# A two-layer trunk on one core: the u projection moved last, compression weights six ahead, phasor sums on VectorE, five projection banks

## The chip, the core and the metric

The kernel runs on one core of a Trainium2 chip. The metric is the device time of one execution in microseconds (us); the kernel before takes 1839.51 us in the median of 3 runs (1838.10 to 1841.22). Each core has a matrix engine (TensorE, PE in the rows), a vector engine (VectorE, DVE), a scalar engine (ScalarE, ACT), GpSimd (POOL) and a sync engine (SP) that issues most loads. Every engine works through its own instructions in order and waits for others at semaphores.

## What is computed

A decoder trunk of two layers on 512 positions of width 1024, in float32. One combined projection feeds three token mixers; their outputs are gated and merged, and an MLP follows:

```python
for l in range(DEPTH):
    h = rmsnorm(x, norm_mix[l])
    proj = h @ w_in[l]
    q_a, kv_a, g_a, q_b, kv_b, u_c, g_m = jnp.split(proj, splits, axis=-1)
    ...
    y_a = nsa_attention(q_a, k_a, v_a, gates_a, nsa_cmp_pos[l], nsa_cmp_w1[l], nsa_cmp_w2[l])
    ...
    y_b = banded_attention(q_b, k_b, kv_b[:, :, 1], B_WINDOW, swa_sinks[l]).reshape(bsz, seq, B_WIDTH)
    y_c = s5_layer(u_c, s5_a_re[l], ...)
    g_m = jax.nn.sigmoid(g_m.reshape(bsz, seq, N_BRANCH, D_MODEL))
    merged = (g_m[:, :, 0] * (y_a @ w_branch_a[l])
              + g_m[:, :, 1] * (y_b @ w_branch_b[l])
              + g_m[:, :, 2] * (y_c @ w_branch_c[l]))
    x = x + merged @ w_out[l]
    h = rmsnorm(x, norm_mlp[l])
    x = x + jnp.square(jax.nn.relu(h @ w_mlp_up[l])) @ w_mlp_down[l]
return rmsnorm(x, norm_final)
```

`nsa_attention` compresses keys and values of overlapping blocks with a small two-layer network (`nsa_cmp_w1`, `nsa_cmp_w2`); `s5_layer` is a diagonal state-space recurrence, whose tables depend on parameters alone.

## The kernel before, in words

Every float32 product is made of three products: both factors are split into a high and a low half (`hh`, `hl` for the activations; `wh`, `wl` for a weight tile). The high half of a weight is a copy by ScalarE (L138, L146). The low half is either a subtraction on VectorE (`split`, L147) or, with `"add"`, the negated weight written by ScalarE (L137) to which an accumulating DMA, issued by GpSimd, adds the weight again (`split_add`, L139). Raw tiles `wr` have 2 buffers, `wh` and `wl` 3 each.

**The front of a layer** is five projections of 512 positions, one after another through `proj_tok` (L584 to L610): wkv01 (keys and values of two branches), wu (input of the recurrence), wkv2 (third branch, gates and the banded keys; 408 columns), wqb and wqa (queries). Each has four weight pieces `kp`; under each piece four tiles of 128 positions `t`; under each of these six matmuls into the tile's PSUM bank (tag `mm`, 4 banks), so one piece is 24 matmuls. After each group of six, `tick()` advances the background generators. At the end the four banks are evacuated: keys and queries by `rope` on VectorE (three operations), values by `v_split`, gates by a tanh on ScalarE, u by a ScalarE copy (L724). The next projection takes the same banks.

**In the background** run three generators. `turn()` transposes the keys and ends in `compress` (L1073 to L1118): 16 small weights `cw`, each for two matmuls of 65 columns into a bank `y`, eight for the keys and eight for the values; after each eight come a gelu and a small second matmul into another bank `y`, copied and split into `kst` or `vcst`. The weights are loaded three ahead into four buffers on SP's queue (`load_cw1`, L1068). In layer 0 `s5_prep` (L434 to L581) builds the tables of the recurrence in four quarters. A quarter has two steps. The first makes `wpn` and `wpnt` (products of powers, 128x1024), joined by an accumulating DMA (L520), and the phasors `E` and `Et` (L533 to L537), joined by another (L538) and stored as `cs`. The second multiplies `wpn` on TensorE (L563), copies it to `wi` and stores it as `win`, and makes `mo` and `mot` (L517, L518), joined and stored. The tiles wpn, wpnt, wi, mo and mot share four buffers (tag `pw`). `PD` gives the ticks: 9 to the start, 16 to the first quarter, 10 between the steps of a quarter; 1 tick lies between two quarters.

Attention follows at once: `q_stack` (L923) copies a query tile to `qd` on ScalarE, transposes it on TensorE, and splits it into `qh` (ScalarE, L933) and `ql` (VectorE, L934); scores and the filling gate matmuls (L153 to L155) come next.

The order on each engine is set by a scheduler when the program is built: it may move an instruction ahead of one that it takes to be late. On the chip each engine keeps that order.

Of the kernel before, what the change touches and what calls it, by code (L numbers as in the profile page):

```python
# [9 lines left out]
F32 = mybir.dt.float32  # L10
# [9 lines left out]
TT = S // 128  # L20
NEG = -1e38
STB = 0
PD = 9, 16, 10
NP = 8
EPS = 1e-6

# [37 lines left out]
class Trunk:  # L64
# [223 lines left out]
        self.yp = self.yp_cm.__enter__()  # L288

    def last_turn(self, tag):  # L290
        self.pins = [self.norm_turn(TT - 1, c, self.xlast[c], tag) for c in range(2)][1]

    def norm_turn(self, t, c, xg, tag):
        nc = self.nc
# [7 lines left out]
    def first_norm(self, pa):  # L302


        nc, I, tc = self.nc, self.I, self.tc
        ctx = ExitStack()
        xp, p = (ctx.enter_context(tc.tile_pool(name=n, bufs=1, reuse_waits="tile")) for n in ("xp", "nrm"))
        self.x = [xp.tile([128, D], F32, name=f"x{t}") for t in range(TT)]
        raw = []
        for t in range(TT):  # L310
            nc.sync.dma_start(self.x[t], I["x"][t * 128:(t + 1) * 128])
            if t == 0:
                self.norm_begin(p, I["norm_mix"][0])
                self.setup()
            elif t < 3:
                raw.append(self.raw(I["wkv01"][0, t - 1], 2, 512))
        nc.sync.dma_start(self.c, I["consts"])

        w = p.tile([128, 512], F32R, name="warm")
        nc.vector.memset(w.bitcast(F32), 0.0)  # L320
        b = self.bank("mm")
        for i in range(12):
            nc.tensor.matmul(b, w[:, 0:128], w, start=i == 0, stop=i == 11)
        xg, pre = [], []

        def gained(t):
            with self.after(self.pins):
                self.norm_sum(t, 0)
                self.norm_sum(t, 1)
                r = self.norm_rstd(t)  # L330
                xg.append([self.norm_half(t, c, r) for c in range(2)])

        def lead(t):
            if t < 2:
                with self.after([self.pow_done]):
                    pre.append(self.split(raw[t], nc.gpsimd))
            self.pins = [i for c in range(2) for i in self.norm_turn(t, c, xg[t][c], "y")] + [self.pow_done]
            if t + 2 < TT:
                gained(t + 2)
            if t == STB:  # L340
                with self.after(self.pins):
                    init.append(next(steps))
            if t == TT - 1:
                ctx.close()
                with self.after(self.pins):
                    self.rope_tables()

        self.pins = []
        gained(0)
        self.pins = [self.xg_done]  # L350
        gained(1)
        init, steps = [], self.s5_init(0, pa)
        with self.after([self.xg_done, self.sq_done]):
            next(steps)
        return lead, pre, init


# [76 lines left out]
    def s5_prep(self, l, init=None):  # L434
# [8 lines left out]
        with tc.tile_pool(name="prep", bufs=1, side="right", reuse_waits="tile") as p:  # L443
# [15 lines left out]

            V.tensor_scalar(PH[:, 1], PH[:, 1], self.sg, None, op0=OP.mult)  # L460
            if acc:
                PN = p.tile([128, 32, 8], F32, name="PN")
                V.tensor_scalar(PN, PH[:, 1, 1], -1.0, None, op0=OP.mult)
                NI = p.tile([128, 9, 32], F32, name="NI")
                V.tensor_scalar(NI, PI, -1.0, None, op0=OP.mult)
            loaded, nl = [], 2
# [15 lines left out]
            for q in range(4):  # L482
# [42 lines left out]
                wp_ = powers((X[:, 0], X[:, 1]), 1, "wpn")  # L525

                E = p.tile([128, 2, 8, 8, 8], F32, name="E", tag="E", bufs=nb)
                Et = p.tile([128, 2, 8, 8, 8] if acc else [128, 8, 8, 8], F32, name="Et", bufs=nb)
                eng = V
                se = [128, 8, 8, 8]  # L530
                hr, hi = (PH[:, x, 1, gs][:, :, :, None].to_broadcast(se) for x in range(2))
                lr, li = (PH[:, x, 0, gs][:, :, None, :].to_broadcast(se) for x in range(2))
                eng.tensor_tensor(E[:, 0], hr, lr, op=OP.mult)  # L533
                eng.tensor_tensor(E[:, 1], hr, li, op=OP.mult)
                if acc:
                    eng.tensor_tensor(Et[:, 0], PN[:, gs][:, :, :, None].to_broadcast(se), li, op=OP.mult)
                    eng.tensor_tensor(Et[:, 1], hi, lr, op=OP.mult)  # L537
                    nc.gpsimd.dma_start(E, Et, accum_op=OP.add)  # L538
                else:
                    eng.tensor_tensor(Et, hi, li, op=OP.mult)  # L540
                    eng.tensor_tensor(E[:, 0], E[:, 0], Et, op=OP.subtract)
                    eng.tensor_tensor(Et, hi, lr, op=OP.mult)
                    eng.tensor_tensor(E[:, 1], E[:, 1], Et, op=OP.add)

                def put(cs_d=cs_d, E=E):
                    nc.gpsimd.dma_start(cs_d, E.rearrange("p two g a b -> p two g (a b)"))

                if not acc:
                    put()
                V.tensor_tensor(ed, ed, self.c[:, None, C_E:C_E + 16].to_broadcast(sh), op=OP.mult)  # L550
                pins.close()
                if q < 3:
                    load(q + 1)
                yield PD[2]
                if acc:
                    put()

                wi = p.tile([128, 8, 128], F32, name="wi", tag="pw" if acc else "wi", bufs=4 if acc else 1)
                for g0 in (0, 3, 6):
# [15 lines left out]
                if not acc:  # L575
                    put()
                    put = lambda: None
                yield 1
            if acc:
                yield PD[2]  # L580
                put()  # L581


# [65 lines left out]
    def mixing(self, l, h):  # L649
        tc = self.tc  # L650
        with ExitStack() as right:
            def pool(name, side="right"):
                return tc.tile_pool(name=name, bufs=1, side=side, reuse_waits="tile")

            if l:
                right.push(self.yp_cm)
            with pool("qkv", "left") as self.qkv:
                with pool("pj", "left") as pj, self.banks(mm=4, s=1, t=1, y=2):
                    merged = self.q_pools(right, pool)
                    if l == 0:  # L660
                        pa = pool("pa")
                        *start, init = self.first_norm(pa.__enter__())
                    else:
                        start = [lambda t: t == TT - 1 and self.last_turn("y")]
                    self.project_init(l, pj)
                    if l == 0:
                        self.spawn(self.s5_prep(0, init), PD[0])
                    self.project_kv01(l, h, pj, *start)
                    self.project_u(l, h, pj)
                    self.project_kv2(l, h, pj)  # L670
                    self.project_qb(l, h, pj)
                    self.project_qa(l, h, pj)
                    self.drain()
                    if l == 0:
                        pa.__exit__(None, None, None)
                        self.y_pool()
                        right.push(self.yp_cm)
                self.ybp = right.enter_context(pool("ybp"))
                yb = [self.ybp.tile([128, 4, S], F32R, name=n, tag=n) for n in ("ybh", "ybl")]
                with pool("att", "left") as p, self.banks(mm=2, s=2, t=2, q=1, y=1):  # L680
                    ga = []
                    fill = self.fill(l, h, yb, merged, ga)
                    ya = self.attention(l, p, yb, self.yp, fill)
                    self.dump(f"yb{l}", yb[0].bitcast(F32))
                    self.dump(f"ya{l}", ya[0].bitcast(F32))
            with pool("post", "left") as p, self.banks(mm=4, s=1, t=1, y=2):
                self.scan_branch(l, h, p, fill, ya, ga, merged)
            with self.banks(mm=8):
                return self.w_out(l)
# [335 lines left out]
    def project_kv01(self, l, h, p, lead=None, pre=()):  # L1025
# [19 lines left out]

        def turn():
            self.cw1 = []
            for w in range(3):
                self.load_cw1(l, p, w)
            for t in range(TT):  # L1050
                kd, v0 = kds[t]
# [14 lines left out]
        self.proj_tok(h, self.I["wqa"][l], 512, self.evac_q(p, "qa"))  # L1066

    def load_cw1(self, l, p, w):  # L1068
        w1 = p.tile([128, 2, 128], F32, name="cw1", tag="cw1", bufs=4)
        self.nc.sync.dma_start(w1, self.I["cw1"][l, w // 8, w // 2 % 4][:, 2 * (w % 2):2 * (w % 2) + 2])  # L1070
        self.cw1.append(w1)

    def compress(self, l, p):  # L1073
# [7 lines left out]
        for j in range(2):  # L1081
            bh = self.bank("y")
            for w in range(8):
                if 8 * j + w < 13:
                    self.load_cw1(l, p, 8 * j + w + 3)
                if w % 2 == 0:
                    yield 2
                w1 = w1s[8 * j + w]
                for i in range(2):
                    ii = 2 * w + i  # L1090
                    nc.tensor.matmul(bh[:, 0:65], w1[:, i], ck[j][:, 2 * ii:2 * ii + 1025:16], start=ii == 0, stop=ii == 15)
# [303 lines left out]
    def mlp(self, l, h):  # L1395
# [3 lines left out]
        with tc.tile_pool(name="mlp", bufs=1, reuse_waits="tile") as p, self.banks(mm=7, t=1):  # L1399
# [3 lines left out]
            for fc in range(4):  # L1403
                act = []
                for f in range(8):
                    if (fc, f) in steps:
                        next(prep, None)
                    if not later:
# [3 lines left out]
                        for a, z in ((0, S - 128), (S - 128, S)) if len(two) > 1 else ((0, S),):  # L1412
                            for w, b in parts:
                                for kt in range(KT):
                                    if z < S and b is parts[1][1] and kt == 3:
                                        self.last_turn("t")
                                    self.mm3(b[:, a:z], (w[0][:, kt], w[1][:, kt]), (h[0][:, kt, a:z], h[1][:, kt, a:z]), kt == 0, kt == KT - 1)
                        later = [b for w, b in parts]
                    b = later.pop(0)
# [124 lines left out]
```

## Time and profile before

| | |
|---|---|
| median of the runs | 1839.51 us (1838.10 to 1841.22) |
| profiled execution, its own time | 1837.11 us |
| its span, first to last instruction | 1835.3 us |
| TensorE busy | 1767.5 us (96%), mean granted clock 0.986 of full speed |
| VectorE / ScalarE / GpSimd busy | 1049.3 us (57%) / 878.1 us (48%) / 149.5 us (8%) |
| DMA | 245.45 MB, mean 134 GB/s |

Busy is the time in which an engine has at least one instruction at work; TensorE's matmuls overlap, so their durations add up to more than the time between their starts. The granted clock is the share of TensorE's 2.4 GHz that the chip let through; its two levels are 2.4 and 1.2 GHz. The front of layer 0 lies between 0 and 185 us, that of layer 1 between about 961 and 1077 us.

### The profile page before, as it was taken

What the parts mean: (1) busy time and instruction counts of PE and PEld (TensorE: products, weight loads), DVE (VectorE), ACT (ScalarE), POOL (GpSimd) and SP (SyncE); (2) the same over time, 40 slices, a digit from 0 to 9 for tenths busy, and PEclk for the clock granted to TensorE, in tenths of its full rate; (3) what the DMA queues carried; (4) which work ended last, traced back from release to release, by engine and by line L of the source; (5) the groups of instructions that cost most, each with busy time, mean ns of one, the idle gap of its engine ahead of it and who ended that gap; (6) DMA issues with size and microseconds to landing.
All of it is one profiled execution on the core that took longest, in us unless ns stands there. A gap on an engine that the chain in (4) does not pass through costs nothing.

```text
span 1835.3 us, 23424 instructions
## 1 busy us (share of the span) xinstructions
PE 1767.5 (96%) x8560; PEld 1460.5 (80%) x8560; DVE 1049.3 (57%) x2606; ACT 878.1 (48%) x1675; POOL 149.5 (8%) x211
## 2 busy tenths in 40 slices
PE   7879999999999999999999999999999999999998
PEld 5777778878888788887888877787888888888887
DVE  7555789957454715161263568897655643434344
ACT  5532888753433635353535349876433332323232
POOL 3121000010001111111100000000100000000000
PEclk8889999999999999999999999999999999999999
DMA  5897444144344889898943345323533523323232
GB/s 180 203 244 195 104 93 104 39 154 133 94 165 111 192 195 244 192 223 192 221 156 94 105 92 115 70 58 104 173 93 103 172 69 99 96 92 103 92 104 80
DMA packets 77106, 245.45 MB, mean 134 GB/s; under 512 B 11072, under 2 KB 17440, under 8 KB 76992
## 3 DMA queue, kind: packets, MB, share of 16 engines
q1 hardware_dynamic: 51344, 156.49, 27.0%
q0 software_dynamic: 24352, 83.02, 22.3%
q10 hardware_dynamic: 1296, 4.46, 0.6%
q8 instruction: 67, 1.10, 0.2%
q14 instruction: 47, 0.39, 0.1%
HBM read 219.88 MB, written 17.76 MB: 129 GB/s over the span
## 4 chain that ended last, share of the span: by engine, by line
PE 83%; DVE 5%; ACT 5%; DMA 4%; issue 2%; POOL 0%; SPq 0%; POOLq 0%; DVEq 0%; ACTq 0%
PE b_mm L153 20%; PE b_mm L154 19%; PE b_mm L155 19%; PE b_mm L607 11%; PE b_t L948 3%; PE b_y L1182 2%; PE b_y L1184 1%; PE b_s L1255 1%; PE b_s L1256 1%; DMA wl<-in_wdn 1%; DMA cw<-in_cw 1%; PE b_y L802 1%; PE b_y L781 1%; PE b_s L778 1%; ACT bP L1151 1%
## 5 line engine op out<-in xcount | busy, mean ns | idle before, releaser
L153 PE MATMUL b_mm<-hh,wh 128*128 128x512 f32 (+2 forms) x928 | 363.8, 392 | 0.5 <-ACT hh L300 0.5
L155 PE MATMUL b_mm<-hh,wl 128*128 128x512 f32 (+2 forms) x928 | 360.3, 388 | 1.5 <-DMA wl<-in_wup 1.5
L154 PE MATMUL b_mm<-hl,wh 128*128 128x512 f32 (+2 forms) x928 | 359.5, 387 | 0.6 <-DVE hl L300 0.6
L147 DVE TENSOR_TENSOR wl<-wr,wh 128x1024 fp32r<-128x1024 f32 (+1 forms) x144 | 175.3, 1218 | 272.9 <-ACT wh L146 272.5
L146 ACT CAST wh<-wr 128x1024 fp32r<-128x1024 f32 (+1 forms) x146 | 152.7, 1046 | 298.9 <-PE b_mm L154 150.2
L155 PEld LDWEIGHTS b_mm<-hh,wl 128*128 128x128 f32 x928 | 174.8, 188 | 35.5 <-DMA wl<-in_wup 3.0
L153 PEld LDWEIGHTS b_mm<-hh,wh 128*128 128x128 f32 x928 | 175.4, 189 | 32.4 <-issue 1.0
L154 PEld LDWEIGHTS b_mm<-hl,wh 128*128 128x128 f32 x928 | 175.4, 189 | 31.3 <-DVE hl L300 1.1
L154 PE MATMUL b_mm<-wl,ah 128*128 128x512 f32 x448 | 174.5, 390 | 2.3 <-DMA wl<-in_wdn 2.3
L155 PE MATMUL b_mm<-wh,al 128*128 128x512 f32 x448 | 174.3, 389 | 0.0
L153 PE MATMUL b_mm<-wh,ah 128*128 128x512 f32 x448 | 174.3, 389 | 0.0
L137 ACT ACTIVATE wl<-wr 128x1024 fp32r<-128x1024 f32 (+1 forms) x98 | 103.0, 1051 | 91.5 <-PE b_mm L154 79.0
L138 ACT CAST wh<-wr 128x1024 fp32r<-128x1024 f32 (+1 forms) x98 | 101.7, 1037 | 83.3 <-PE b_mm L154 58.0
L630 DVE TENSOR_TENSOR x<-b_mm,x 128x512 f32<-128x512 f32 x79 | 53.7, 689 | 129.5 <-PE b_mm L155 128.4
L607 PE MATMUL b_mm<-wh,hh 128*128 128x512 f32 (+1 forms) x320 | 105.6, 413 | 11.2 <-ACT gates L1011 4.7
L607 PE MATMUL b_mm<-wh,hl 128*128 128x512 f32 (+1 forms) x320 | 102.7, 400 | 4.3 <-DVE hl L300 4.3
L154 PEld LDWEIGHTS b_mm<-wl,ah 128*128 128x128 f32 x448 | 84.1, 188 | 20.6 <-DMA wl<-in_wdn 3.2
L607 PE MATMUL b_mm<-wl,hh 128*128 128x512 f32 (+1 forms) x320 | 100.0, 396 | 0.0
L155 PEld LDWEIGHTS b_mm<-wh,al 128*128 128x128 f32 x448 | 84.1, 188 | 17.5
L153 PEld LDWEIGHTS b_mm<-wh,ah 128*128 128x128 f32 x448 | 84.1, 188 | 17.4
L950 ACT CAST pth<-b_t 128x512 fp32r<-128x512 f32 x124 | 69.9, 586 | 44.1 <-PE b_t L948 41.9
L607 PEld LDWEIGHTS b_mm<-wh,hh 128*128 128x128 f32 x320 | 64.8, 218 | 22.0 <-ACT gates L1011 5.6
(359 smaller groups left out, 3251.8 us busy)
## 6 DMA issues: line engine op xcount, KB each, us to landing
wr<-in_wup SPq DMA_DIRECT2D x64, 512.0 KB, 3.9
wr<-in_wdn SPq DMA_DIRECT2D x64, 512.0 KB, 4.1
wr<-in_wg SPq DMA_DIRECT2D x48, 512.0 KB, 3.7
wl<-in_wup POOLq DMA_DIRECT2D x32, 512.0 KB, 7.3
wl<-in_wdn POOLq DMA_DIRECT2D x28, 512.0 KB, 7.4
wr<-in_wp SPq DMA_DIRECT2D x24, 512.0 KB, 3.5
wl<-in_wg POOLq DMA_DIRECT2D x22, 512.0 KB, 5.9
wr<-in_wo SPq DMA_DIRECT2D x16, 512.0 KB, 3.5
```

What stands on the lines that cost most here:

```text
L137: nc.scalar.activation(lo, raw, AF.Copy, scale=-1.0)
L138: nc.scalar.copy(hi, raw)
L146: nc.scalar.copy(hi, raw)
L147: (eng or nc.vector).tensor_tensor(lo, raw, hi.bitcast(F32), op=OP.subtract)
L153: mm(out, ah, bh, start=start, stop=False)
L154: mm(out, ah, bl, start=False, stop=False)
L155: mm(out, al, bh, start=False, stop=stop)
L607: nc.tensor.matmul(banks[t][:, 0:n], part(a, kt, ts), w[b][:, k], start=kt == 0 and b == 0 and a is hh, stop=kt == KT - 1 and b == 1)
L630: self.nc.vector.tensor_tensor(o, bank, o, op=OP.add)
L948: nc.tensor.transpose(b[:, i * 128:(i + 1) * 128], x, self.ident)
L950: nc.scalar.copy(ph, b)
L1182: mm(by, v, ph, start=first, stop=end and pl is None)
```

## The change

It has five parts. (1) In both layers u is projected after wqa, as the last of the five. (2) Compression weights are loaded six ahead into eight buffers, and a step of two weights comes every 3 ticks instead of 2. (3) In layer 0 the two sums of the phasors are made by VectorE, the negated table `PN` and the accumulating DMA fall away, `Et` is halved, and `cs` is stored at once. (4) The projections have five `mm` banks and one `y` bank instead of four and two; the norm's transposes take `y` and `t` in turn. (5) `PD` gives 7 ticks between the steps of a quarter and 5 between quarters.

```diff
-PD = 9, 16, 10
+PD = 9, 16, 7, 5
...
-            self.pins = [i for c in range(2) for i in self.norm_turn(t, c, xg[t][c], "y")] + [self.pow_done]
+            self.pins = [i for c in range(2) for i in self.norm_turn(t, c, xg[t][c], "yt"[c])] + [self.pow_done]
...
             if acc:
-                PN = p.tile([128, 32, 8], F32, name="PN")
-                V.tensor_scalar(PN, PH[:, 1, 1], -1.0, None, op0=OP.mult)
...
-                Et = p.tile([128, 2, 8, 8, 8] if acc else [128, 8, 8, 8], F32, name="Et", bufs=nb)
+                Et = p.tile([128, 8, 8, 8], F32, name="Et", bufs=nb)
...
                 eng.tensor_tensor(E[:, 0], hr, lr, op=OP.mult)
+                eng.tensor_tensor(Et, hi, li, op=OP.mult)
+                eng.tensor_tensor(E[:, 0], E[:, 0], Et, op=OP.subtract)
                 eng.tensor_tensor(E[:, 1], hr, li, op=OP.mult)
-                if acc:
-                    eng.tensor_tensor(Et[:, 0], PN[:, gs][:, :, :, None].to_broadcast(se), li, op=OP.mult)
-                    eng.tensor_tensor(Et[:, 1], hi, lr, op=OP.mult)
-                    nc.gpsimd.dma_start(E, Et, accum_op=OP.add)
...
-                def put(cs_d=cs_d, E=E):
-                    nc.gpsimd.dma_start(cs_d, E.rearrange("p two g a b -> p two g (a b)"))
...
+                eng.tensor_tensor(Et, hi, lr, op=OP.mult)
+                eng.tensor_tensor(E[:, 1], E[:, 1], Et, op=OP.add)
+                nc.gpsimd.dma_start(cs_d, E.rearrange("p two g a b -> p two g (a b)"))
...
                 yield PD[2]
-                if acc:
-                    put()
...
-                yield 1
+                yield PD[3]
             if acc:
-                yield PD[2]
                 put()
...
-                with pool("pj", "left") as pj, self.banks(mm=4, s=1, t=1, y=2):
+                with pool("pj", "left") as pj, self.banks(mm=5, s=1, t=1, y=1):
...
-                    self.project_u(l, h, pj)
                     self.project_kv2(l, h, pj)
                     self.project_qb(l, h, pj)
                     self.project_qa(l, h, pj)
+                    self.project_u(l, h, pj)
...
-            for w in range(3):
+            for w in range(6):
                 self.load_cw1(l, p, w)
...
-        w1 = p.tile([128, 2, 128], F32, name="cw1", tag="cw1", bufs=4)
+        w1 = p.tile([128, 2, 128], F32, name="cw1", tag="cw1", bufs=8)
...
-                if 8 * j + w < 13:
-                    self.load_cw1(l, p, 8 * j + w + 3)
+                if 8 * j + w < 10:
+                    self.load_cw1(l, p, 8 * j + w + 6)
                 if w % 2 == 0:
-                    yield 2
+                    yield 3
```

How the order on the engines moves is shown at three places. The first is SP's queue in the front of layer 0, where the compression weights cw (numbered by the program) stand among the raw loads `wr`. Before, the fifth to eleventh of sixteen:

```order
L124 DMA wr_882<-in_wkv2 128x816
L124 DMA wr_986<-in_wkv2 128x816
L124 DMA wr_1029<-in_wkv2 128x816
L1070 DMA cw1_744<-in_cw1 128x256
L1070 DMA cw1_748<-in_cw1 128x256
L1070 DMA cw1_802<-in_cw1 128x256
L1070 DMA cw1_806<-in_cw1 128x256
L1070 DMA cw1_822<-in_cw1 128x256
L1070 DMA cw1_826<-in_cw1 128x256
L124 DMA wr_1072<-in_wkv2 128x816
L1070 DMA cw1_849<-in_cw1 128x256
```

Now the ninth to the last, the first eight having been issued before wkv2's first raw load:

```order
L124 DMA wr_1106<-in_wqb 128x1024
L124 DMA wr_1181<-in_wqb 128x1024
L1055 DMA cw1_798<-in_cw1 128x256
L1055 DMA cw1_820<-in_cw1 128x256
...
L1055 DMA cw1_983<-in_cw1 128x256
L124 DMA wr_1244<-in_wqa 128x1024
L469 DMA bc_1050<-in_s5bc 128x512
L554 DMA kd00_759<-ed_500 8x16x128
L1055 DMA cw1_1065<-in_cw1 128x256
L1055 DMA cw1_1121<-in_cw1 128x256
```

The later weights moved behind all four raw loads of wqb, and the last two also behind wqa's first, a load of `bc` and a store of `kd`.

The second place is VectorE at the evacuation of wkv2 in layer 0 (`ropa`, `ropb`, `kd`, `v`, `vb` and `gates` are the evacuation, `wpn` and `wpnt` belong to `s5_prep`, `kst` is the keys' transpose). Before:

```order
L517 TENSOR_TENSOR wpn<-XX,PR 128x1024
L941 TENSOR_TENSOR v_200<-b_mm,v_200 128x2x64
L643 TENSOR_TENSOR ropb<-b_mm,rsin 128x128
L997 TENSOR_TENSOR kst_202<-b_s,kst_202 64x128
L646 TENSOR_TENSOR kd<-ropa,ropb 128x128
L941 TENSOR_TENSOR vb<-b_mm,vb 128x64
L518 TENSOR_TENSOR wpnt<-XX,PI 128x1024
L1012 TENSOR_SCALAR gates<-gates 128x24
```

Now:

```order
L515 TENSOR_TENSOR wpn<-XX,PR 128x1024
L926 TENSOR_TENSOR vb<-b_mm,vb 128x64
L627 TENSOR_TENSOR ropa<-b_mm,rcos 128x64
L628 TENSOR_TENSOR ropb<-b_mm,rsin 128x64
L516 TENSOR_TENSOR wpnt<-XX,PI 128x1024
L997 TENSOR_SCALAR gates<-gates 128x24
L631 TENSOR_TENSOR kd<-ropa,ropb 128x64
L926 TENSOR_TENSOR v_200<-b_mm,v_200 128x2x64
```

Behind these rows stand the rest of the evacuation, the six operations on E and Et, and the read of the first compression result out of `y` (L1091). The `wpnt` amid the evacuation now stands behind two of its four banks and belongs to the second quarter; before, it stood behind the first bank and belonged to the third.

The third place is VectorE at the end of the front of layer 0. Before:

```order
L642 TENSOR_TENSOR ropa<-b_mm,rcos 128x512
L643 TENSOR_TENSOR ropb<-b_mm,rsin 128x512
L646 TENSOR_TENSOR qa_1650<-ropa,ropb 128x512
L934 TENSOR_TENSOR ql<-b_q,qh 128x512
L1144 ISA bP,bm<-b_s,consts,sk 128x128
```

Now:

```order
L631 TENSOR_TENSOR qa_1492<-ropa,ropb 128x512
L515 TENSOR_TENSOR mo<-ZI,PR 128x1024
L553 TENSOR_TENSOR ed<-ed,b_t 128x48
L553 TENSOR_TENSOR ed<-ed,b_s 128x48
L516 TENSOR_TENSOR mot<-bc,NI 128x1024
L553 TENSOR_TENSOR ed<-ed,b_t 128x32
L919 TENSOR_TENSOR ql<-b_q,qh 128x512
```

The ropes of wqa moved away from the first query's low half; the fourth quarter's second step, which falls into the projection of u, stands between them.

## Rows read from the trace of the kernel before

**Rows 1.** Stretches: length, PE, PEld, DVE, ACT, POOL busy, PEclk, DMA share, GB/s.

```profile
45.00:88.00 43.00, 34.35 (x143) 30.43 (x142) 23.46 (x79) 24.04 (x64) 7.42 (x9) 0.88 0.87 208
88.00:125.00 37.00, 29.57 (x170) 28.83 (x168) 17.10 (x41) 11.33 (x20) 8.51 (x11) 0.86 0.92 235
125.00:158.00 33.00, 27.35 (x119) 21.26 (x118) 20.88 (x64) 13.61 (x33) 6.80 (x9) 0.95 0.93 238
158.00:185.00 27.00, 26.22 (x116) 21.38 (x116) 17.04 (x26) 4.59 (x8) 2.28 (x3) 0.94 0.67 159
185.00:193.00 8.00, 3.89 (x17) 3.41 (x17) 5.86 (x17) 6.38 (x12) 0.85 (x1) 0.80 0.59 133
...
1077.00:1088.00 11.00, 6.89 (x27) 5.68 (x27) 7.87 (x25) 8.34 (x18) 0.86 (x1) 0.69 0.59 143
```

**Rows 2.** Timeline of TensorE, layer 1, wqb's start: start, duration, line, tile, count [idle before].

```profile
1031.94 0.73 PE L607 MATMUL b_mm<-wh,hh 128*128 128x512 f32 x2 [1.48 <-ACT gates L1011]
```

**Rows 3.** Waits of TensorE, 40 to 210 us: waiter, releaser, us in total, times, longest.

```profile
PE b_y L1091 <- DMA cw<-in_cw: 11.7, 2, 7.4
PE b_s L1141 <- DVE ql L934: 3.4, 1, 3.4
PE b_mm L607 <- ACT gates L1011: 3.2, 2, 3.0
PE b_mm L607 <- DVE ropb L643: 3.1, 1, 3.1
PE b_s L987 <- DVE kd L646: 1.9, 1, 1.9
```

**Rows 4.** Timeline of TensorE, layer 0, around the two waits for cw.

```profile
78.27 1.12 PE L1091 MATMUL b_y<-ck,cw 128*128 128x65 f32 x4 [4.26 <-DMA cw<-in_cw]
...
82.71 1.05 PE L607 MATMUL b_mm<-wh,hl 128*128 128x512 f32 x2
...
87.16 0.63 PE L607 MATMUL b_mm<-wh,hl 128*128 128x512 f32 x2
...
111.66 1.97 PE L1091 MATMUL b_y<-ck,cw 128*128 128x65 f32 x8 [7.43 <-DMA cw<-in_cw]
```

**Rows 5.** Timeline of SP's queue, layer 0: start, length, load, count.

```profile
70.68 10.35 SPq L1070 DMA_DIRECT2D cw<-in_cw  x6
```

**Rows 6.** DMA, 40 to 186 us: a queue (packets, MB, share); loads (count, KB, median landing).

```profile
q0 software_dynamic: 4752, 16.88, 55.0%
...
wl<-in_wu POOLq DMA_DIRECT2D x4, 512.0 KB, 9.1
...
win<-wi ACTq DMA_DIRECT2D x4, 512.0 KB, 6.8
...
wl<-in_wqb POOLq DMA_DIRECT2D x4, 512.0 KB, 7.5
...
wl<-in_wkv POOLq DMA_DIRECT2D x4, 408.0 KB, 8.1
...
cw<-in_cw SPq DMA_DIRECT2D x12, 128.0 KB, 5.4
```

**Rows 7.** Timeline of POOL, layer 0: accumulates of u's low halves as issued.

```profile
40.70 0.96 POOL L139 DMA_DIRECT2D wl<-in_wu  x1 [9.50 <-DVE ang L183]
...
62.83 0.85 POOL L139 DMA_DIRECT2D wl<-in_wu  x1 [12.98 <-ACT wl L137]
```

**Rows 8.** Waits of VectorE, 40 to 186 us.

```profile
DVE Et L536 <- DMA E<-Et: 11.2, 2, 5.7
...
DVE wpnt L518 <- DMA win<-wi: 2.4, 1, 2.4
```

**Rows 9.** Timeline of VectorE, layer 0: a product of the phasors.

```profile
62.30 0.68 DVE L533 TENSOR_TENSOR E<-PH 128x512 f32<-128x512 f32 x1
```

**Rows 10.** Tile wpn, 40 to 170 us: landing of its accumulates.

```profile
DMA to landing us min/median/max: 4.5/7.6/10.2
```

**Rows 11.** Timeline of VectorE, layer 0, start of attention.

```profile
188.86 0.68 DVE L934 TENSOR_TENSOR ql<-b_q,qh 128x512 fp32r<-128x512 f32 x1
```

More of the change, by code (lines that the diff above doesn't have):

```diff
@@ L290, in last_turn @@
     def last_turn(self, tag):
-        self.pins = [self.norm_turn(TT - 1, c, self.xlast[c], tag) for c in range(2)][1]
+        self.pins = [self.norm_turn(TT - 1, c, self.xlast[c], tag[c]) for c in range(2)][1]
     def norm_turn(self, t, c, xg, tag):
@@ L533, in s5_prep @@
                 eng.tensor_tensor(E[:, 0], hr, lr, op=OP.mult)
+                eng.tensor_tensor(Et, hi, li, op=OP.mult)
+                eng.tensor_tensor(E[:, 0], E[:, 0], Et, op=OP.subtract)
                 eng.tensor_tensor(E[:, 1], hr, li, op=OP.mult)
-                if acc:
-                    eng.tensor_tensor(Et[:, 0], PN[:, gs][:, :, :, None].to_broadcast(se), li, op=OP.mult)
-                    eng.tensor_tensor(Et[:, 1], hi, lr, op=OP.mult)
-                    nc.gpsimd.dma_start(E, Et, accum_op=OP.add)
[L539 to L543, printed above, removed]
-                def put(cs_d=cs_d, E=E):
-                    nc.gpsimd.dma_start(cs_d, E.rearrange("p two g a b -> p two g (a b)"))
-                if not acc:
-                    put()
+                eng.tensor_tensor(Et, hi, lr, op=OP.mult)
+                eng.tensor_tensor(E[:, 1], E[:, 1], Et, op=OP.add)
+                nc.gpsimd.dma_start(cs_d, E.rearrange("p two g a b -> p two g (a b)"))
                 V.tensor_tensor(ed, ed, self.c[:, None, C_E:C_E + 16].to_broadcast(sh), op=OP.mult)
@@ L554, in s5_prep @@
                 yield PD[2]
-                if acc:
-                    put()
                 wi = p.tile([128, 8, 128], F32, name="wi", tag="pw" if acc else "wi", bufs=4 if acc else 1)
@@ L663, in mixing @@
                     else:
-                        start = [lambda t: t == TT - 1 and self.last_turn("y")]
+                        start = [lambda t: t == TT - 1 and self.last_turn("yt")]
                     self.project_init(l, pj)
@@ L1415, in mlp @@
                                     if z < S and b is parts[1][1] and kt == 3:
-                                        self.last_turn("t")
+                                        self.last_turn("tt")
                                     self.mm3(b[:, a:z], (w[0][:, kt], w[1][:, kt]), (h[0][:, kt, a:z], h[1][:, kt, a:z]), kt == 0, kt == KT - 1)
```

## The prediction

> **What bounds the kernel now.** The page shows TensorE busy 96% of the span, so a gain can only come from where it stands or runs slowly. The stretches by window show where that is. In the front of layer 0 (the five projections) it is busy 34.35 of 43 us, 29.57 of 37, 27.35 of 33 and 26.22 of 27, and 3.89 of the 8 us in which attention begins [rows 1]: 26.6 us idle. The mean granted clock there is 0.88, 0.86, 0.95, 0.94 and 0.80. Layer 1's front stands only where attention begins, 4.1 of 11 us at a clock of 0.69 [rows 1], and for 1.5 us ahead of its fourth projection [rows 2].
>
> The view of waits names what TensorE waited for in layer 0's front [rows 3]: 11.7 us for compression weights (cw) from a DMA, 3.2 for the gates' evacuation on ScalarE and 3.1 for a rope on VectorE (both hold banks of the projection before), 1.9 for the first evacuation's ropes, 3.4 for the low half of the first query. After a long wait the clock is at its lower level, 1.2 GHz, for a while: after the 4.26 us wait at 78.27, a pair of 512-column matmuls still takes 1.05 us at 82.71, and 0.63 again at 87.16; the 7.43 us wait is the other long one [rows 4]. I read six slow microseconds after each, of which half is lost. The 1.48 us wait is followed by a pair of 0.73 us, at full clock [rows 2].
>
> **The change, part by part,** against the profiled execution: span 1835.3, time 1837.1 us.
>
> *Compression weights six ahead in eight buffers.* Before, the fifth weight and those after it wait in SP's queue until TensorE has released a buffer: six such loads are issued from 70.68 to 81.0 us [rows 5], and a load then takes 5.4 us to land [rows 6]. With eight buffers, the first eight weights are loaded before the second projection's own. Saved: the 11.7 us, and 3.0 us of half clock twice: **17.7 us**. What is late next: weights 9 to 14 stand in SP's queue behind all four raw loads of wqb. The last of those needs only a buffer two pieces back, some 50 matmuls (12 us) ahead of the use; I price it at nothing.
>
> *First boundary, now wkv01 to wkv2.* The fifth bank lets TensorE go on without an evacuation. But the second projection's first low half is an accumulating DMA, issued at 40.70 [rows 7]; such loads landed after 9.1 us for wu and 8.1 for wkv2 [rows 6], so at about 49, as late as the evacuation. The 1.9 us there shrink only by four matmuls done early: **1.0 saved**.
>
> *Second boundary, now wkv2 to wqb.* Here I expect more waiting. The third pass of wqb needs a bank that ScalarE releases only behind the first half's gelu; I put that at 2.0 us. The fourth needs one whose evacuation on VectorE stands behind the second quarter's `wpnt`, which waits for the store of `wi`, 6.8 us to landing [rows 6]: 3.6 us. Such a wait was 2.4 us before, in the same evacuation [rows 8]; now the store comes sooner before it. With 2.0 of half clock that makes 7.6 us, against 3.2 idle and 1.7 half clock before (0.95 over 33 us): **2.7 lost**.
>
> *Third boundary, wqb to wqa.* Before, 3.1 idle and 1.6 half clock (0.94 over 27 us). The fifth bank gives one pass more, and no store is near: 0.5 left, **4.2 saved**. *New small waits:* wqa's ropes hold banks of u (1.2), the low halves of u's second piece (1.0) and of wkv2's last (0.7), and wqa's splits on VectorE behind the sums (1.0), each put at the size of the 0.7 to 1.9 us that such waits have here: **3.9 lost**.
>
> *The phasor sums.* Two sums of 128x512 in each of four quarters, as long as the product of that shape (0.68 us [rows 9]): 5.5 us on VectorE. In exchange it loses two waits for the accumulate, 11.2 us [rows 8], so on the path this is nothing; if that cover goes, up to 5.5. Four accumulates leave the DMA engines: queue 0 moves 16.88 MB in 55.0% of 146 us [rows 6], 4.8 us a MB, so these 2.1 MB are some 10 us of the engines' time.
>
> POOL issued a weight's accumulate in 0.85 us at 62.83, while VectorE ran such a product of two SBUF operands, and in 0.96 us at 40.70 [rows 7, 9]. The Trainium skill (SBUF — State Buffer, section Who interferes with whom) warns that VectorE and GpSimd contend for a shared port. By that rule the eight sums could hold POOL's issues back, and the gain would be up to 5.5 us smaller. The trace does not bear it out, and I keep nothing for it.
>
> *Crowding.* The same transfers fall into a shorter time, at a share of 0.92 and 0.93 already [rows 1]. I charge one accumulate that lands after the longest 10.2 instead of the median 7.6 us [rows 10], and 0.9 of clock: **3.5 lost**.
>
> *Start of attention.* Before, the first query's low half `ql` starts at 188.86 [rows 11], right behind four ropes of wqa, and TensorE stands until then. With u last, VectorE is free, and five gate matmuls stand ahead of most scores. ScalarE still copies u and splits a weight ahead of `qh`, so I leave 1.3 us. Layer 0: 4.1 idle and 1.6 half clock (0.80 over 8 us), less 1.3: **4.4 saved**. Layer 1: 4.1 idle and 2.6 half clock (0.69 over 11 us is 3.4 at most), less 1.3: **5.4 saved**. The fifth bank takes 1.3 of layer 1's 1.5 us, and wkv2 right behind wkv01 costs 0.5: **0.8 saved**.
>
> *One y bank instead of two.* The compression's second half must wait until VectorE has read the first half's result; that read stands behind wkv2's evacuation, the second quarter's products and its sums, about 18 us of work, and TensorE comes there some 25 us after wkv2. Nothing is lost; a late VectorE (B below) would use that slack up first.
>
> Sum: 17.7 + 1.0 - 2.7 + 4.2 - 3.9 - 3.5 + 4.4 + 5.4 + 0.8 = 23.4 us. The profiled execution would take 1813.7; the median of the runs stands 2.4 us above it: **1816.1 us**. Bounds: with the three lost terms gone (10.1) the gain is 33.5; with the weights or VectorE late it loses 9 to 12.
>
> **The rivals.**
>
> A. *The accumulating weights become the bound.* A piece's slot is free three pieces back; then come two passes on ScalarE, the issue (0.85 us [rows 7]) and the landing (7.5 to 8.1 [rows 6]), some 11 us in all. Two pieces of 24 matmuls at 0.23 us (116 in 26.22 us [rows 1]) are 11 us of TensorE, and of 408 columns (408/512 of that) less than 9. For it: a share of 0.93. Against: other matmuls lie between, and four accumulates are gone. Eight pieces late by 1.5 us (a bit over half of 10.2 - 7.6) are 12 us: 1828 us. The Trainium skill (DMA: Bandwidth & Descriptors, section Issuing engines are not separate DMA queues) says that loads from several engines run on the same 16 DMA engines and interleave; by that rule an earlier issue buys no bandwidth, and the share of 0.93 agrees. Chance 0.20.
>
> B. *VectorE holds the banks at the second boundary.* If the store lands after 10.2 us (as wpn's longest) instead of 6.8, and the sums' 5.5 us come onto the path, 9 us are lost: 1825 us. For it: VectorE waited for transfers of both kinds [rows 8]. Against: the stores were never that late. Chance 0.10. A and B together take nearly all: 1837 us, no change. Chance 0.05.
>
> C. *SP's queue brings the cw waits back (slower).* Weights 9 to 16 stand behind wqb's raw loads, wqa's first, a bc load and a kd store, each waiting for another engine. If one of these holds SP, each of four pairs stalls TensorE as the two did, (4.26 + 7.43) / 2 + 3.0 = 8.9 us. Four pairs are 35.6 us more: 1852 us. It decides from the third pair on, when the 23.4 us are used up. For it: this queue did that before [rows 5]; against: the raw loads need ScalarE only. Chance 0.06.
>
> D. *The new waits do not come.* 33.5 us saved: 1806 us. The DMA engines' time (84% of 146 us less 10, or 113 us) would allow it. Chance 0.09.
>
> **How the numbers follow.** The forecast (1809 to 1823) has 0.50, the others as given. 1804 to 1831 takes in the forecast, A, B and D, nominally 0.89, with their own spread about 0.8. Within 0.2% (3.7 us, about what a measurement can tell) lies A with B: same 0.06, slower 0.06, faster 0.88.
>
> **What would show it.** Right: no wait of TensorE for cw; no accumulate into E; attention's first query near 172 us instead of 184.5; under 1.5 us idle there in both layers, at full clock in layer 1; waits of 3 to 6 us for VectorE or ScalarE at the start of wqb. Wrong: over 5 us of waits for `wl` of wqb or wu (A), a wait of VectorE above 6 us for the `wi` store (B), a wait for cw in the middle of wqb (C).

## The result and the profile after

The changed kernel takes 1816.73 us in the median of 4 runs (1813.28 to 1818.11), the one before 1839.4 beside it: a ratio of 0.9873 (95% interval 0.9856 to 0.9890), 22.7 us less. The forecast was 1816.1. The profiled execution of the changed kernel takes 1816.53 us, with a span of 1814.7 us against 1835.3.

Where the 20.6 us of span went is read from one line of code, the projections' matmul (L607, now L592). The view of one source line gives count, shortest, median and longest ns, and the first and last start. Before:

```profile
L607 PE MATMUL b_mm<-wl,hh x160: 344/389/632, 17.3 to 184.2; 128*128 128x512 f32 x128, 128*128 128x408 f32 x32
...
L607 PE MATMUL b_mm<-wh,hh x160: 344/389/632, 954.4 to 1076.1; 128*128 128x512 f32 x128, 128*128 128x408 f32 x32
```

After, the same two, of layer 0 and of layer 1:

```profile
L592 PE MATMUL b_mm<-wl,hh x160: 341/392/632, 17.6 to 172.0; 128*128 128x512 f32 x128, 128*128 128x408 f32 x32
...
L592 PE MATMUL b_mm<-wh,hh x160: 344/389/501, 940.2 to 1061.4; 128*128 128x512 f32 x128, 128*128 128x408 f32 x32
```

Layer 0's front ends at 172.0 instead of 184.2: 12.2 us. From there to layer 1's first projection it was 770.2 us and is 768.2: 2.0 us. From that projection to the end of the span it was 880.9 and is 874.5: 6.4 us. The forecast's terms, put to the same three places, are 12.8, 4.4 and 6.2: near at the first and the last, more than twice too high at the second.

The stretches by window that answer to [rows 1], in the same columns:

```profile
45.00:88.00 43.00, 36.34 (x194) 31.60 (x192) 29.62 (x104) 27.07 (x73) 7.02 (x9) 0.96 0.88 226
88.00:125.00 37.00, 31.78 (x152) 26.40 (x153) 30.98 (x72) 10.83 (x28) 5.64 (x8) 0.91 0.64 171
125.00:158.00 33.00, 30.26 (x138) 25.75 (x137) 24.82 (x45) 11.62 (x17) 6.79 (x9) 0.95 0.89 248
158.00:185.00 27.00, 24.72 (x107) 22.85 (x105) 4.88 (x27) 14.80 (x29) 3.40 (x5) 0.87 0.84 208
...
960.00:1077.00 117.00, 112.06 (x565) 98.59 (x563) 60.31 (x162) 55.62 (x136) 2.63 (x3) 1.00 0.37 104
```

TensorE still stands for 14.6 us between 45 and 158 (21.7 before), and the last stretch now holds layer 1's front and the start of its attention, at full clock. The waits of TensorE that answer to [rows 3] say for what:

```profile
PE b_mm L592 <- ACT gates L996: 4.2, 1, 4.2
PE b_s L972 <- ACT ck L1020: 2.5, 3, 1.1
PE b_mm L592 <- DMA wl<-in_wkv: 2.4, 1, 2.4
PE b_s L972 <- DVE kstb L982: 2.4, 1, 2.4
PE b_mm L155 <- DMA wl<-in_wg: 2.3, 1, 2.3
PE b_mm L592 <- DVE ropb L628: 2.2, 2, 2.0
PE b_mm L592 <- DMA wl<-in_wu: 0.5, 1, 0.5
```

The 11.7 us for cw are gone, and so are the 3.4 us for `ql`. The largest that is left, 4.2 us for the gates, is the second boundary as forecast. The timelines of VectorE and of TensorE there:

```profile
88.31 1.22 DVE L516 TENSOR_TENSOR wpnt<-XX,PI 128x1024 f32<-128x1024 f32 x1 [4.46 <-DMA win<-wi]
```

```profile
90.75 1.22 PE L592 MATMUL b_mm<-wh,hh 128*128 128x512 f32 x2 [4.16 <-ACT gates L996]
```

The evacuation stands behind `wpnt`, which waits for the store of `wi`; ScalarE's last gate activation and TensorE follow. Two waits were not forecast. At 107.92 the keys' transpose waits 2.4 us for `kstb`, because VectorE, ahead of it, may not write E until the store of `cs` has landed (2.62 us, at 104.82). And attention begins with a wait for a gate weight's low half. TensorE, then GpSimd's queue:

```profile
175.63 0.79 PE L155 MATMUL b_mm<-hh,wl 128*128 128x512 f32 x1 [2.28 <-DMA wl<-in_wg]
```

```profile
157.42 0.84 POOL L518 DMA_DIRECT2D mo<-mot  x1 [1.27 <-DVE mot L516]
167.72 0.56 POOL L559 DMA_DIRECT2D md<-mo  x1 [9.46 <-DMA mo<-mot]
168.27 1.76 POOL L139 DMA_DIRECT2D wl<-in_wg  x2
```

GpSimd waits 9.46 us to store the last quarter's `md`, since `mo` is still being accumulated, and two gate weights stand behind that store.

### The profile page after: what moved, and what is told of

Its sections match the earlier page's. It is cut to its first block, busy times and chain, and to the rows that moved or that the text cites. A ratio compares the mean times of both kernels' runs of the same rounds, so it can differ in the third digit from the quotient of the medians.

```text
span 1814.7 us, 23427 instructions
## 1 busy us (share of the span) xinstructions
PE 1761.5 (97%) x8560; PEld 1456.1 (80%) x8560; DVE 1053.2 (58%) x2613; ACT 879.6 (48%) x1677; POOL 145.8 (8%) x207
## 3 DMA queue, kind: packets, MB, share of 16 engines
q10 hardware_dynamic: 1296, 4.46, 0.6%
## 4 chain that ended last, share of the span: by engine, by line
PE 81%; DMA 6%; ACT 5%; DVE 3%; issue 3%; POOL 0%; POOLq 0%; ACTq 0%; DVEq 0%
PE b_mm L155 20%; PE b_mm L153 19%; PE b_mm L154 19%; PE b_mm L592 9%; PE b_t L933 3%; PE b_y L1167 2%; DMA wl<-in_wup 1%; PE b_y L1169 1%; PE b_s L1240 1%; PE b_s L1241 1%; DMA wl<-in_wdn 1%; DMA wr<-in_wu 1%; PE b_y L787 1%; PE b_y L766 1%; PE b_s L763 1%
## 5 line engine op out<-in xcount | busy, mean ns | idle before, releaser
L592 PE MATMUL b_mm<-wh,hh 128*128 128x512 f32 (+1 forms) x320 | 103.8, 407 | 8.7 <-ACT gates L996 4.2
L592 PE MATMUL b_mm<-wh,hl 128*128 128x512 f32 (+1 forms) x320 | 100.9, 395 | 4.2 <-DVE hl L300 4.2
L592 PE MATMUL b_mm<-wl,hh 128*128 128x512 f32 (+1 forms) x320 | 100.6, 396 | 3.1 <-DMA wl<-in_wkv 2.4
L1409 DVE TENSOR_TENSOR rel<-b_mm,rel 128x512 f32<-128x512 f32 x64 | 43.9, 685 | 65.7 <-ACT rel L1408 65.7
```

The costliest lines, as they stand in the source:

```text
L592: nc.tensor.matmul(banks[t][:, 0:n], part(a, kt, ts), w[b][:, k], start=kt == 0 and b == 0 and a is hh, stop=kt == KT - 1 and b == 1)
L1409: nc.vector.tensor_tensor(r, b, r, op=OP.mult)
```

## The experiments: what each part is worth

Each part of the change was made or undone by itself. The forecast had given a price to each part; these runs show whether the price belongs to the part.

**The sums alone** (before, with the phasors as in the change):

```diff
-                    nc.gpsimd.dma_start(E, Et, accum_op=OP.add)
+                eng.tensor_tensor(E[:, 0], E[:, 0], Et, op=OP.subtract)
...
+                eng.tensor_tensor(E[:, 1], E[:, 1], Et, op=OP.add)
```

> The kernel before (1839.4 us) with the phasors' sums on VectorE alone, the negated table and the accumulate gone and cs stored at once. Theory (nothing on the path: VectorE loses 11.2 us of waits and gains 5.5 us of work): 1837 to 1841 us. Rival 1 (2.1 MB fewer through the DMA engines, some 10 us of their time, bring cw and the rest earlier): waits for cw fall below 8 us, 1828 to 1836 us. Rival 2 (the sums come onto the path): 1842 to 1846 us.

Measured: 1837.90 us, ratio 0.9987 (0.9975 to 0.9998), 2.3 us less than the 1840.17 beside it, hardly clear of noise. The waits for cw stay, 11.2 us in three. The sums cost nothing, as forecast.

**The sums and the weights' buffers** (before, with cw six ahead in eight buffers and a step every 3 ticks as well; without the sums, Et and PN take that room):

```diff
-        w1 = p.tile([128, 2, 128], F32, name="cw1", tag="cw1", bufs=4)
+        w1 = p.tile([128, 2, 128], F32, name="cw1", tag="cw1", bufs=8)
...
-                    self.load_cw1(l, p, 8 * j + w + 3)
+                    self.load_cw1(l, p, 8 * j + w + 6)
```

> The kernel before with the phasors' sums on VectorE (1837.9 us by the run of that part alone) and, in the room that they free, the compression weights six ahead in eight buffers, a step every 3 ticks. Theory 1 (the forecast's term: the waits for cw are worth 17.7 us by themselves): no wait for cw, 1818 to 1823 us. Theory 2 (the run of the changed kernel with four buffers lost nothing: where the weights stop being late, something else of the same queues is, and the order of the projections decides): the waits for cw go, others of 5 us or more for wpn, wl or the evacuations come, 1826 to 1836 us.

Measured: 1827.13 us, ratio 0.9935 (0.9921 to 0.9948): 10.8 us less than the sums alone, not 17.7. TensorE's waits show what came instead:

```profile
PE b_t L549 <- DVE ed L553: 4.5, 2, 2.8
PE b_mm L593 <- ACT gates L997: 4.1, 2, 3.3
PE b_t L549 <- DMA wpn<-wpnt: 3.7, 2, 2.6
```

None is for cw. In place of those TensorE waits for the tables: 8.2 us for `wpn` and for the bank that `ed` holds. Theory 2 holds.

**The changed kernel without the weights' buffers** (three ahead, four buffers, a step every 2 ticks; all else changed):

> The changed kernel (1816.7 us) with the compression weights as before: three ahead, four buffers, a step of two every 2 ticks. Theory (the weights' waits were worth 17.7 us: 11.7 idle and 6 of half clock): TensorE waits for cw again, 10 us or more in layer 0, and the kernel takes 1831 to 1842 us; the weights from the fifth on stand behind all four raw loads of wqb on SP's queue, so rather the upper half. Rival (with u last and four accumulates fewer the DMA engines would have delivered four buffers' weights in time too): under 3 us of waits for cw, 1816 to 1821 us.

Measured: 1817.37 us, ratio 0.9876 (0.9862 to 0.9889), as the full change. The forecast's largest term is worth nothing here. TensorE's waits in the trace of this version:

```profile
PE b_s L972 <- DVE kstb L982: 5.7, 2, 4.6
PE b_t L549 <- DMA wpn<-wpnt: 3.1, 2, 2.6
...
PE b_y L1076 <- DMA cw<-in_cw: 2.1, 1, 2.1
```

Of the cw waits only 2.1 us come back, though the weights stand behind wqb's raw loads. TensorE stands 4.6 us for `kstb` at 99.04 instead, while the next weights land. That wait comes from VectorE, where the change's own wait (the 4.46 us above) has another place and another transfer:

```profile
93.51 1.23 DVE L516 TENSOR_TENSOR wpnt<-XX,PI 128x1024 f32<-128x1024 f32 x1 [6.01 <-DMA mo<-mot]
```

**u last alone** (before, with the call of `project_u` moved behind `project_qa`):

> The kernel before with u projected last and nothing else. Theory 1 (the forecast's terms: u last is worth the two starts of attention, 4.4 + 5.4 us, and the waits for cw stay): over 8 us of waits for cw, 1828 to 1832 us. Theory 2 (u last also brings the compression ahead of u's four accumulating weights and so takes the waits for cw away, which is why the changed kernel with four weight buffers has only 2.1 us of them): under 4 us of waits for cw, 1814 to 1823 us.

Measured: 1829.91 us, ratio 0.9948 (0.9932 to 0.9965): 9.9 us less than the 1839.79 beside it. The time is theory 1's (forecast 9.8 for the two starts of attention), the waits are not:

```profile
PE b_y L1091 <- DMA cw<-in_cw: 5.2, 1, 5.2
PE b_mm L607 <- DVE ropb L643: 4.7, 2, 2.9
PE b_s L987 <- DVE kstb L997: 4.3, 1, 4.3
PE b_mm L607 <- DMA wl<-in_wkv: 2.9, 1, 2.9
```

The cw waits halve, and others come. Layer 0's front ends later than the 184.2 of before:

```profile
L607 PE MATMUL b_mm<-wl,hh x160: 342/389/775, 17.1 to 188.3; 128*128 128x512 f32 x128, 128*128 128x408 f32 x32
```

Layer 1's first projection starts at 953.7, against 954.4. So from the front's end on layer 0 wins 4.8 us, near the forecast's 4.4, but the front gives 4.1 of them back; layer 0 as a whole wins 0.7.

**The changed kernel with u second again:**

> The changed kernel with u projected second again. Theory (u last is worth what the two starts of attention cost before: 4.1 us idle and 1.6 to 2.6 of half clock in each layer; forecast 4.4 + 5.4 us, of which the trace after shows 2.0 in layer 0 and 5.9 in layer 1): TensorE waits over 2.5 us for ql in both layers, 1823 to 1828 us. Rival (what u last saves at the start of attention it gives back at the boundaries of the front, where wqa's ropes and the weight wl of wkv2 are waited for): 1815 to 1820 us.

Measured: 1824.07 us, ratio 0.9915 (0.9902 to 0.9927), 7.3 us more than the change; the two intervals are apart. `ql` is waited for again, 3.4 us in each layer. The source line of the projections, layer 1, in this version and in the one with u last alone:

```profile
L592 PE MATMUL b_mm<-wh,hh x160: 344/389/602, 942.2 to 1063.3; 128*128 128x512 f32 x128, 128*128 128x408 f32 x32
```

```profile
L607 PE MATMUL b_mm<-wh,hh x160: 341/389/497, 953.7 to 1074.2; 128*128 128x512 f32 x128, 128*128 128x408 f32 x32
```

With spans of 1822.3 and 1827.9 us, the rest of the program from there takes 880.1 with u second and 874.2 with u last, beside 880.9 before and 874.5 after. So of layer 1's 6.4 us the other parts bring 0.8 without u last, and u last brings 5.6 on top of them and 6.7 alone. This is the one gain that stays nearly the same whatever else is changed: read the same way in all 14 traces of this document, that stretch takes 879.7 to 881.3 us in the four with u second and 873.7 to 874.9 in the ten with u last. Within the ten, the five with four banks take 873.7 to 874.2 and the five with five banks 874.5 to 874.9: in layer 1 the fifth bank gains nothing.

**The sums and u last:**

> The kernel before with u last and the phasors' sums on VectorE, and neither the weights' six ahead, nor the fifth bank, nor the new ticks. u last alone takes 1829.9 us, the sums alone 1837.9, together by addition 1828. Theory 1 (u last and the sums are what takes the weights' waits away in the changed kernel with four weight buffers, 1817.4 us): under 4 us of waits for cw, 1814 to 1821 us. Theory 2 (the fifth bank and the new ticks do it, a step of which was undone alone without loss only because the other stood in): over 5 us of waits for cw, 1825 to 1831 us.

Measured: 1827.46 us, ratio 0.9928 (0.9909 to 0.9947). Theory 2's time: the two parts add up (1828 was the sum), though the waits for cw, 4.7 us, stay just under its 5. The largest waits are others:

```profile
PE b_t L549 <- DMA wpn<-wpnt: 7.2, 2, 6.6
PE b_mm L593 <- DVE ropb L629: 5.3, 2, 4.1
PE b_y L1077 <- DMA cw<-in_cw: 4.7, 2, 3.8
```

**Four banks, two y banks** in the changed kernel, and **the old ticks** in it:

```diff
-                with pool("pj", "left") as pj, self.banks(mm=5, s=1, t=1, y=1):
+                with pool("pj", "left") as pj, self.banks(mm=4, s=1, t=1, y=2):
```

```diff
-PD = 9, 16, 7, 5
+PD = 9, 16, 10, 1
```

> The changed kernel with four mm and two y banks, the norm's transposes in y again. Theory (the fifth bank is worth about one pass at each boundary: 3.1 us at wqb to wqa, 1.3 in layer 1, and 1 to 2 at each other boundary): the waits of TensorE's projections for evacuations grow by 4 to 9 us, 1820 to 1828 us. Rival (the banks come free behind the same VectorE work, and the late weights bound the boundaries anyway): 1815 to 1819 us.

> The changed kernel with the ticks of before: 10 between the steps of a quarter and 1 between quarters, instead of 7 and 5. Theory (the ticks move the second quarter's store of wi to just before the evacuation of wkv2, a 4.2 us wait at wqb's start that other ticks would not have): that wait goes, others come in its place, 1811 to 1819 us. Rival (the even spread is what keeps VectorE from holding banks, a part of the gain that I had not priced): 1822 us or more.

Measured: 1810.79 us, ratio 0.9846 (0.9831 to 0.9861) with four banks; 1817.59 us, ratio 0.9879 (0.9866 to 0.9893) with the old ticks. The interval of four banks overlaps with the change's only at its edge: the fifth bank gains nothing in this setting and may cost up to 6 us. Both theories on it fall, and why four banks should be faster stays open: the execution that was traced took 1816.55 us, as long as the changed kernel, and none near the median of 1810.79 has a trace. The old ticks take away most of the gates' wait (1.3 us instead of 4.2) and bring others, as the theory said:

```profile
PE b_s L972 <- DVE kstb L982: 6.2, 2, 5.9
PE b_t L549 <- DMA wpn<-wpnt: 5.3, 1, 5.3
```

Weights' buffers, fifth bank and new ticks thus cost nothing when one of them is undone. When all three are, with u last and the sums kept, the time is 1827.46 instead of 1816.73.

## The experiments: what the waits hang on

**The last quarter's mo summed by VectorE**, on the version with four banks:

```diff
-                    if acc:
+                    if acc and not sm:
                         nc.gpsimd.dma_start(o, tm, accum_op=OP.add)
                     else:
-                        V.tensor_tensor(o, o, tm, op=sign)
+                        V.tensor_tensor(o, o, tm, op=OP.add if acc else sign)
...
-                mo = powers((ZI[:, :, 128:144], Z2), 0, "mo", OP.subtract)
+                mo = powers((ZI[:, :, 128:144], Z2), 0, "mo", OP.subtract, acc and q == 3)
```

> The changed kernel with four mm and two y banks (1810.8 us) and, in the last quarter, mo and mot summed by VectorE (1.2 us, where it stands idle) instead of joined by an accumulating DMA. Theory (the first gate weights' low halves are late because GpSimd, before it issues them, waits 9 to 11 us for that accumulate to land, with the store of md): the 3.6 us wait for wl of wg and the half clock behind it go, 1804 to 1808 us. Rival (those weights are late by themselves, since their raw loads land late at a DMA share near 1): the wait stays over 2 us, 1809 to 1813 us.

Measured: 1813.07 us, ratio 0.9853 (0.9840 to 0.9866). The cause is shown for the trace, a gain in time is not. GpSimd now issues `md` at once and the gate weights from 163.91 on, and this wait of TensorE, from the trace with four banks, is gone:

```profile
PE b_mm L155 <- DMA wl<-in_wg: 3.6, 1, 3.6
```

GpSimd's queue in the new version:

```profile
157.96 0.87 POOL L559 DMA_DIRECT2D md<-mo  x1
163.91 0.84 POOL L139 DMA_DIRECT2D wl<-in_wg  x1 [5.08 <-ACT wl L137]
```

From the front's end to layer 1's first projection it is 764.5 us, against 769.2 in the trace with four banks, so the wait and the half clock behind it were worth something there. Yet the median is that of four banks alone within the intervals. Whether the executions near 1810.79 us had the wait at all, no trace shows.

**Where the weights' 4 KB go instead.** On the changed kernel with four weight buffers (1817.37 us), the room went once into a fifth buffer for the tag `pw`, once into a second one for E:

```diff
-                    o = p.tile([128, 8, 8, 16], F32, name=name, tag="pw", bufs=4 if acc else 2)
+                    o = p.tile([128, 8, 8, 16], F32, name=name, tag="pw", bufs=5 if acc else 2)
```

> The changed kernel with four weight buffers again (1817.4 us so) and, in the 4 KB that they leave free, a fifth buffer for wpn, wpnt, wi, mo and mot. Theory 1 (VectorE's waits for the stores and accumulates that hold these buffers, 8.4 us with four, reach TensorE through the work queued behind them): TensorE's waits for kstb and wpn, 5.7 and 3.1 us, fall by half, 1810 to 1814 us. Theory 2 (any one wait that goes in this front gives its time to the next, as with the weights): 1815 to 1819 us.

```diff
-                E = p.tile([128, 2, 8, 8, 8], F32, name="E", tag="E", bufs=nb)
+                E = p.tile([128, 2, 8, 8, 8], F32, name="E", tag="E", bufs=2)
```

> The changed kernel with four weight buffers again (1817.4 us so) and a second buffer for E instead. Theory 1 (VectorE's wait for the store of cs, 4.1 us there and 7.6 with the old ticks, is what holds the keys' transposes back: TensorE's wait for kstb): the waits for kstb fall under 2 us, 1810 to 1814 us. Theory 2 (the wait goes to the next in line): 1815 to 1819 us.

Measured: 1816.25 us, ratio 0.9871 (0.9846 to 0.9896) with the fifth `pw`; 1811.50 us, ratio 0.9843 (0.9819 to 0.9867) with the second E. The fifth `pw` does what was expected of it: `kstb` falls from 5.7 to 2.3 us, `wpn` from 3.1 to 0.4. The time goes to the next in line (theory 2):

```profile
PE b_mm L155 <- DMA wl<-in_wg: 3.8, 1, 3.8
PE b_y L1076 <- DMA cw<-in_cw: 3.4, 2, 3.0
PE b_s L972 <- DVE kstb L982: 2.3, 1, 2.3
```

With the second E the wait for `kstb` is gone altogether, and the time is 5.9 us lower (theory 1's time), though the intervals meet at 0.9862 to 0.9867. Theory 1's cause holds for a part of those waits. With four weight buffers and one E, VectorE and TensorE stood here:

```profile
106.73 0.69 DVE L531 TENSOR_TENSOR E<-PH 128x512 f32<-128x512 f32 x1 [3.82 <-DMA cs<-E]
109.82 0.41 PE L972 MATMUL b_s<-ident,kd 128*128 128x128 f32 x2 [1.11 <-DVE kstb L982]
```

Only this shorter wait for `kstb` stood behind the store of `cs`; the 4.6 us stood behind `wpnt`'s 6.01 us wait for `mo`. With the fifth `pw` that wait of `wpnt` is gone, and the 2.3 us for `kstb` that are left stand behind E's wait for `cs` (2.66 us). With the second E the latter is gone, and `wpnt` waits 0.85 us for `mo`; why so little stays open. TensorE's largest waits are then:

```profile
PE b_y L1076 <- DMA cw<-in_cw: 4.6, 2, 3.1
PE b_s L972 <- ACT ck L1020: 2.3, 3, 1.1
PE b_mm L592 <- DMA wl<-in_wkv: 1.9, 1, 1.9
```

**The second E with four banks:** of the change u last, the sums and the new ticks are left.

> The version with four weight buffers and two buffers for E (1811.5 us) and also four mm and two y banks: of the change there remain u last, the sums on VectorE and the new ticks. Without the new ticks, and with one buffer for E, these parts take 1827.5 us (waits for cw 4.7, wpn 7.2, kstb 5.0, ropb 5.3 us). Theory 1 (the new ticks, which spread a quarter's two steps evenly, stand in for the weights' buffers and the fifth bank): 1806 to 1813 us, ropb and wpn under 3 us together. Theory 2 (the fifth bank does it): those waits come back, less some 6 us for E's second buffer, 1819 to 1824 us.

Measured: 1817.45 us beside 1841.93 for the kernel before, ratio 0.9869 (0.9849 to 0.9889). It lies between the theories. `ropb` is not waited for without the fifth bank, which speaks for the ticks, but cw (5.4 us, once) and `wpn` (5.1) are. Which of ticks and bank stands in for the weights' buffers stays open. Of all versions the two at 1811 us (four banks; a second E in place of the weights' buffers) have the lowest medians; their intervals overlap with the change's, so that neither is shown to be better.

## Why the prediction was right, point by point

The total holds, and of its three places the first and the last: 12.8, 4.4 and 6.2 us forecast, 12.2, 2.0 and 6.4 measured. What was said of the mechanism holds in part, and that the sum came out so close is in good part luck. The single steps:

- *Compression weights, 17.7.* The waits are gone from the trace, as forecast; the price is not the part's. On top of the sums alone it brought 10.8 us, and undone in the changed kernel it cost nothing. The step that failed is "Saved: the 11.7 us, and 3.0 us of half clock twice", which took what TensorE waits for as what the wait's removal gives. Where the weights alone were mended, TensorE waited for the tables instead; where they were not, it stood for `kstb` while weights landed. Which of the late ones is waited for depends on the others.
- *First boundary, 1.0.* The accumulating weight is late, as said: 2.4 us, where 3.0 stood before (`kd` and `v`). Saved 0.6.
- *Second boundary, 5.6 us of waiting.* 4.2. The wait behind `wpnt` and the store of `wi` came (4.46, forecast 3.6), the 2.0 behind the gelu did not.
- *Third boundary and new small waits.* No wait is left at wqa's start. At u's start 2.2 for the ropes and 0.5 for `wl` (forecast 1.2 and 1.0). The splits of wqa (1.0) and wkv2's last low half (0.7) were not waited for; the keys' transposes were, for `ck` 2.5 and `kstb` 2.4.
- *The sums, 0.* Alone a ratio of 0.9987. The rule that the prediction weighed (the Trainium skill, SBUF — State Buffer, section Who interferes with whom) does not show in the time: GpSimd issues the accumulates between 45 and 160 in 0.83 to 0.89 us, as before; two that take 1.15 and 1.17 start before the one ahead has ended. The issue at 95.46 takes 0.85 us beside a sum of E at 95.78. The same section says that `tensor_tensor`, the operation of these sums, was not seen to stall a DMA; the trace agrees. VectorE's 11.2 us of waits for the accumulate are gone, and of its waits for the store of `cs` 2.6 us are left of 3.5. But now TensorE stands 2.4 us for `kstb` behind that store, which it did not before, and the text named no work queued there.
- *Start of attention, 4.4 and 5.4.* The first query's transposes stand at 172.28 (forecast 172). In layer 1 they stand at 1062.60, TensorE waits 1.0 us for `qh` there and 0.6 for `bP`, at the edge of the 1.5 forecast, and the clock is full. In layer 0 the 1.3 us left for `qh` were 2.3 for a gate weight, with half clock after it: 2.4 us less than forecast. The sign "under 1.5 us idle there in both layers" did not come in layer 0. GpSimd's queue at the end of the front was the place not looked at.
- *Fifth bank in layer 1, 0.8.* The 1.5 us wait ahead of wqb is gone, but it is gone too where u last was the only change, with four banks. The traces with five banks gain nothing there.
- *Crowding, 3.5.* No run shows this term by itself. The landings did get longer: 8.4 us for `wpn` instead of 7.6, in the median, and 10.5 for u's low halves instead of 9.1.
- *Rivals.* A: `wl` was waited for 2.9 us in all by wkv2 and u, not 12. B: 4.46 us for the store, not 6. C: no wait for cw. D: several of the new waits came.

In sum the errors met: too much for the weights and for the start of attention in layer 0, too much loss for the gelu, and nothing for how the parts help each other. u last and the sums without the other parts leave 1827.46 us, in the trace with layer 0's front ending at 191.7, later than before; the other three, of which any one can be missing, take some 20 us off that front. A list of waits by place gave the total here by errors that met; it did not give the parts.

## What to carry to other kernels

Price a wait by what would be waited for next, not by its length: where several producers are late together, removing one can give less than it was priced at (10.8 of 17.7 us here), and undoing one can cost nothing. A gain at a place where little else is late (u last in layer 1, 5.6 us beside the other parts and 6.7 alone, forecast 5.4) comes near its price; that the free queues there are the reason is argued, not shown. When a store leaves from a single buffer, look at what stands behind the next write to it; and look at the queue of the engine that issues, where an early store that waits holds the loads behind it.

## What was not expected of the hardware

The loss of clock does not follow the length of the wait. After the 4.16 us wait at 90.75 a pair of matmuls is back at 0.62 us at 94.03. After the 2.28 us wait at 175.63 four transposes still take 1.08 us at 179.10, and 0.60 only at 183.39. The stretch by window, and the transposes in the timeline of TensorE:

```profile
176.00:183.00 7.00, 7.00 (x29) 6.18 (x28) 2.22 (x12) 2.75 (x7) 0.00 (x0) 0.54 0.87 221
```

```profile
179.10 1.08 PE L914 MATMUL b_q<-ident,qd 128*128 128x128 f32 x4
...
183.39 0.60 PE L914 MATMUL b_q<-ident,qd 128*128 128x128 f32 x4
```

TensorE is busy all the 7 us at a granted clock of 0.54, near its lower level of 1.2 GHz, after a wait half as long. In the version with four banks a wait of 3.59 us at the same place is followed by 7 us at a granted clock of 0.76; with the fifth `pw` it is 3.76 us, and 7 us at 0.56. So the six slow microseconds that the forecast gave every long wait fit neither the short spells nor the long ones.
